# Fourteen of 22 inner tiles of the first feed-forward layer by seven block products instead of eight

## The chip, the cores and the metric

The kernel runs on one core of a Trainium2 chip. Its engines are TensorE (PE, with its weight loads shown apart as PEld), VectorE (DVE), ScalarE (ACT), GpSimd (POOL) and SyncE (SP), each with an instruction queue of its own; SP, ACT and POOL can also issue DMAs. The time is the device time of one launch in microseconds; less is better.

## The reference

Four layers work on a residual stream `x` of 512 tokens and 1024 features, each on an RMS norm of it: a Conformer convolution module, a feed-forward layer (the one that is changed), four-head retention with rotary positions, and a second feed-forward layer. All is float32.

```python
def conv_ffn(x, w_in, dw_w, dw_b, w_out):
    h = x @ w_in                          # 1024 -> 2 x 2816
    a, u = jnp.split(h, 2, axis=-1)
    a = causal_dwconv(a, dw_w, dw_b)      # three taps along the tokens
    return (jax.nn.silu(a) * u) @ w_out   # 2816 -> 1024

h = rmsnorm(x, norm_ffn_g[i])
x = x + conv_ffn(h, ffn_w_in[i], ffn_dw_w[i], ffn_dw_b[i], ffn_w_out[i])
```

The retention layer turns its queries and keys by `cos` and `sin` of position times inverse frequency, two tables of 128 x 512.

## The kernel before

The stream lies transposed in SBUF, as eight tiles `xT` of 128 features x 512 tokens. Every float32 product is made as three products in the format fp32r: a factor is split into a high part (cast to fp32r) and a low part (the rest), and `mm3` adds high x high, low x high and high x low into one PSUM bank (lines L272 to L274 when a helper of the scheduler records them, and L279 to L283 in the conv layer). Of the weights, ACT makes the high part `wh` (L229) and DVE the low part `wl` (L233), 128 x 1024 at a time, from a raw chunk `wr` of 128 x 2048 (1 MB) that SP's queue loads. `wr`, `wh` and `wl` have four buffers each. `weights()` gives the factors of one chunk (a "unit") to the products and emits the split of the unit after it.

The inner width 2816 of a feed-forward layer is 22 tiles of 128. `HALVES` cuts them in two groups, 0 to 12 and 12 to 22. `ffn_half` takes the tiles of a group: per tile f one bank `fa` and one bank `fu`, each of 8 blocks of features x 3 matmuls with all 512 tokens moving, so 48 matmuls a tile and 96 for a pair of tiles, which shares two chunks of weights. The norm's factor per token is not in the moving factor `n1x` (only the gain is): it is multiplied in when a bank is emptied (`evac`, L811 to L820):

- `ap` = `fa` x `n1r` on DVE (L812), after POOL has zeroed two columns ahead of it (L811);
- the last tap with bias on ACT (L814), the two others on DVE (L815, L816), silu on ACT (L817), times `n1r` on POOL (L818);
- `fy` = `fu` x `ft` on DVE (L820), and its split into `y…h` on ACT (L348) and `y…l` on DVE (L349).

After each group `proj_out` multiplies the `y` tiles by `ffn_w_out` (banks `fo`) and DVE adds the result to `xT` (L430).

The norm's sums are made while the conv layer's output products (`co`, partly with 256 tokens a matmul) run: ACT squares each new `xT` tile (L379), POOL adds six of the eight squares (L380, `n1acc`), and a short chain gives the factor per token: `n1v` on DVE (L330), a power on POOL (L314, `n1y`), a diagonal on DVE (L336, `n1d`), two products that spread it over all partitions (L339, bank `n1b`) and an ACT copy to `n1r` (L341). `n1b` stands among the first products of the layer.

`rotary_tables` (L843 to L877) is a generator. The first feed-forward layer steps it once per tile, behind that tile's L818 and L820. Nearly all of its instructions are POOL's.

The order of the instructions on each engine is set by the Tile framework's scheduler, from its own estimates; `tc.issue_after(i)` keeps an instruction behind another. Heads 1 to 3 of the retention layer already make their values and gates by seven products, with weight sums added by DVE (L255).

Of the kernel before, what the change touches and what calls it, by code (L numbers as in the profile page):

```python
# [74 lines left out]
def _chunks():  # L75


    out, blocks = [], []
# [70 lines left out]
def trunk(ctx, tc, xt_d, positions, ret_gn_g, final_g, weights_d, cols_d, mats_d, ident_d, decay_d, invf_d, out):  # L149
# [30 lines left out]
    chunks, squares = _chunks()  # L180
    descs = [(nk, sum(n for _, n in ranges)) for _, _, _, nk, ranges in chunks]

    units, i = [], 0
    while i < len(descs):
        units += [(i, n) for n in range(7)] if i in squares else [(i, None)]
        i += 4 if i in squares else 1
# [248 lines left out]
    ss0 = sp.tile([P, 1], F32, tag="ss0", bufs=1, name="ss0")
    with conv_scope:
# [298 lines left out]
        def step_v(_, half):  # L735
# [6 lines left out]
            for i in range(KD):  # L742
# [18 lines left out]
                latest[0] = act.copy(hi, c)  # L761
# [20 lines left out]
        proj_out(zs, "co", n1, between=lambda k: run(SEQ_OUT.get(k, "")))  # L782


    def ffn_half(fp, l, norm, f0, f1, hooks=(), side=None):
# [18 lines left out]
        def evac(f):  # L804
            pa, pu = mid.pop(f)

            def wc(j):
# [5 lines left out]
            t = fp.tile([P, S], F32, tag="ft", bufs=3, name=f"ft{l}_{f}")  # L813
            act.activation(t, ap[:, 2:], AF.Identity, scale=wc(2), bias=wc(3))  # L814
            dve.scalar_tensor_tensor(out=t, in0=ap[:, 1:1 + S], scalar=wc(1), in1=t, op0=ALU.mult, op1=ALU.add)  # L815
            dve.scalar_tensor_tensor(out=t, in0=ap[:, 0:S], scalar=wc(0), in1=t, op0=ALU.mult, op1=ALU.add)  # L816
            act.activation(t, t, AF.Silu)  # L817
# [15 lines left out]
    cos = cp.tile([P, S], F32, name="cos")
    sin = cp.tile([P, S], F32, name="sin")

    def rotary_tables(rp):

        posi = rp.tile([P, S], I32, tag="r0", name="posi")
        act.dma_start(posi, positions.partition_broadcast(P))
        invf = cp.tile([P, 1], F32, name="invf")  # L840
        act.dma_start(invf, invf_d)
        ang = rp.tile([P, S], F32, tag="r1", name="ang")
        pool.tensor_copy(ang, posi)  # L843
        pool.tensor_scalar(out=ang, in0=ang, scalar1=invf, scalar2=None, op0=ALU.mult)
        c = [rp.tile([P, S], F32, tag=f"rc{j}", name=f"rc{j}") for j in range(3)]
        dve.tensor_scalar(out=c[0].bitcast(I32), in0=ang.bitcast(I32), scalar1=-65536, scalar2=None, op0=ALU.bitwise_and)
        pool.tensor_tensor(out=ang, in0=ang, in1=c[0], op=ALU.subtract)
        dve.tensor_scalar(out=c[1].bitcast(I32), in0=ang.bitcast(I32), scalar1=-65536, scalar2=None, op0=ALU.bitwise_and)
        pool.tensor_tensor(out=c[2], in0=ang, in1=c[1], op=ALU.subtract)
        q = inv_two_pi_parts()  # L850
        turn = rp.tile([P, S], F32, tag="r2", name="turn")
        p = rp.tile([P, S], F32, tag="r0", name="prod")
        n = rp.tile([P, S], F32, tag="r1", name="near")

        def turns(dst, src):
            pool.tensor_scalar(out=n, in0=src, scalar1=MAGIC, scalar2=-MAGIC, op0=ALU.add, op1=ALU.add)  # L856
            pool.tensor_tensor(out=dst, in0=src, in1=n, op=ALU.subtract)

        yield
        first = True  # L860
        for j, parts in ((0, 4), (1, 3), (2, 3)):
            for i in reversed(range(parts)):
                pool.tensor_scalar(out=p, in0=c[j], scalar1=q[i], scalar2=None, op0=ALU.mult)
                if (i, j) == (0, 0):
                    turns(p, p)
                if first:
                    turns(turn, p)
                    first = False
                else:
                    turns(p, p)  # L870
                    pool.tensor_tensor(out=turn, in0=turn, in1=p, op=ALU.add)
                yield
        turns(turn, turn)
        act.activation(sin, turn, AF.Sin, scale=TWO_PI)
        pool.tensor_scalar(out=turn, in0=turn, scalar1=0.25, scalar2=None, op0=ALU.add)
        turns(turn, turn)
        act.activation(cos, turn, AF.Sin, scale=TWO_PI)  # L877
# [416 lines left out]
```

## Time and profile before

| what | value |
|---|---|
| time, median of 3 runs | 1293.81 us (1292.75 to 1294.05) |
| the profiled execution's own time | 1293.24 us |
| its span in the profile | 1291.5 us |
| granted TensorE clock, mean | 0.999 of full speed |
| first of the conv layer's output products `co` | 136.2 us from the span's start |
| first and last start of the first feed-forward layer's `fa` products (their first block of features) | 182.3 and 477.9 us |

A row of the timeline gives the start, the duration, the engine, the line, the operation, out<-in and, in brackets, the idle time of the engine just before and what ended it. A row of the groups gives line, engine, operation, out<-in, the count, the summed time in us with the mean in ns, and the idle time ahead of it. PE's matmuls overlap, so the rate is read from their starts and not from their durations.

### The profile page before, as it was taken

The numbers are of one execution on the slowest core, as the hardware profiler recorded it, in microseconds if no ns is written. First come the engines' busy times: TensorE is split into PE (matmuls) and PEld (weight loads), VectorE is DVE, ScalarE is ACT, GpSimd is POOL, SyncE is SP. The second block draws the span as 40 slices with busy tenths as digits, with TensorE's granted clock in tenths as the row PEclk, the third lists the DMA queues.
The fourth block names the chain that finished last, engine by engine and source line by source line (L and its number), as shares of the span: only waits on it lengthen the run. The fifth ranks groups of instructions, "written<-read, shape, count | busy, mean of one in ns | idle before, by whom it ended". The sixth has DMA issues, their size and how long they took to land.

```text
span 1291.5 us, 15110 instructions
## 1 busy us (share of the span) xinstructions
PE 1282.0 (99%) x5955; PEld 1067.0 (83%) x5955; DVE 810.0 (63%) x1036; ACT 520.9 (40%) x703; POOL 355.2 (28%) x305
## 2 busy tenths in 40 slices
PE   9999999999999999999999999999999999999997
PEld 7889988888888888888888888878888888888886
DVE  6998657665335554579696596596675643355542
ACT  6646644333124333334435335354443431233332
POOL 0957323797006110221311312304211110011111
PEclk9999999999999999999999999999999999999999
DMA  9533422313221313323314405323224342213111
GB/s 330 225 123 106 148 98 70 127 66 130 98 98 66 130 49 114 131 81 106 106 42 160 138 14 180 103 83 116 97 76 145 94 143 98 98 66 131 33 65 65
DMA packets 35926, 140.48 MB, mean 109 GB/s; under 512 B 10896, under 2 KB 15760, under 8 KB 21776
## 3 DMA queue, kind: packets, MB, share of 16 engines
q1 hardware_dynamic: 32256, 134.02, 30.2%
q10 hardware_dynamic: 3600, 5.52, 1.5%
q8 instruction: 46, 0.75, 0.2%
q14 instruction: 24, 0.20, 0.0%
HBM read 130.08 MB, written 2.10 MB: 102 GB/s over the span
## 4 chain that ended last, share of the span: by engine, by line
PE 96%; DVE 2%; issue 1%; ACT 0%; POOL 0%; POOLq 0%
PE fa L272 6%; PE fa L274 6%; PE fu L273 6%; PE fu L272 6%; PE fu L274 6%; PE fa L273 6%; PE lo L272 3%; PE fo L273 3%; PE fo L274 3%; PE lo L273 3%; PE lo L274 3%; PE fo L272 3%; PE cph L539 2%; PE ro L272 2%; PE ro L273 2%; PE ro L274 2%
## 5 line engine op out<-in xcount | busy, mean ns | idle before, releaser
L233 DVE TENSOR_TENSOR wl<-wr,wh 128x1024 fp32r<-128x1024 f32 (+2 forms) x242 | 302.7, 1254 | 207.2 <-ACT wh L229 203.7
L229 ACT CAST wh<-wr 128x1024 fp32r<-128x1024 f32 (+2 forms) x244 | 250.5, 1029 | 372.0 <-PE fo L274 82.7
L811 POOL MEMSET ap<- 128x2 f32 x44 | 4.2, 99 | 371.7 <-DVE ft L816 305.4
L988 POOL TENSOR_TENSOR gg<-gg,gn 128x512 f32<-128x512 f32 x16 | 27.5, 1719 | 179.3 <-ACT gg L987 179.3
L820 DVE TENSOR_TENSOR fy<-fu,ft 128x512 f32<-128x512 f32 x44 | 30.4, 690 | 68.6 <-PE fu L274 35.0
L814 ACT ACTIVATE ft<-ap,prm 128x512 f32<-128x512 f32 x44 | 35.8, 814 | 71.3 <-DVE ap L812 71.3
L588 DVE SCALAR_TENSOR_TENSOR tp<-hp,prm,tp 128x512 f32<-128x512 f32 x80 | 55.8, 747 | 0.4
L579 POOL TENSOR_TENSOR pla<-pla,plt 128x512 f32<-128x512 f32 x36 | 49.1, 1365 | 9.8 <-ACT pla L575 5.7
L815 DVE SCALAR_TENSOR_TENSOR ft<-ap,prm,ft 128x512 f32<-128x512 f32 x44 | 37.2, 844 | 17.7 <-ACT ft L814 17.5
L817 ACT ACTIVATE ft<-ft 128x512 f32<-128x512 f32 x44 | 27.9, 633 | 45.0 <-DVE ft L816 44.6
L972 POOL TENSOR_TENSOR rs<-rs 128x512 f32<-128x512 f32 x16 | 24.7, 1559 | 67.5 <-DVE rs L971 43.7
L818 POOL TENSOR_TENSOR ft<-ft,n3r 128x512 f32<-128x512 f32 x22 | 32.1, 1461 | 29.0 <-ACT ft L817 29.0
L818 POOL TENSOR_TENSOR ft<-ft,n1r 128x512 f32<-128x512 f32 x22 | 31.6, 1434 | 28.8 <-ACT ft L817 28.8
L816 DVE SCALAR_TENSOR_TENSOR ft<-ap,prm,ft 128x512 f32<-128x512 f32 x44 | 35.8, 814 | 1.5
L578 ACT ACTIVATE plt<-hp,prm 128x512 f32<-128x512 f32 x36 | 25.8, 722 | 20.6 <-POOL pla L579 20.2
L539 PEld LDWEIGHTS cph<-ph,cmat 128*128 128x128 f32 x288 | 32.6, 192 | 0.2
L539 PE MATMUL cph<-ph,cmat 128*128 128x128 f32 x288 | 32.6, 275 | 0.0
L430 DVE TENSOR_TENSOR xT<-ro,xT 128x512 f32<-128x512 f32 x32 | 21.6, 682 | 15.6 <-PE ro L274 15.6
L255 DVE TENSOR_TENSOR wr<-wr,wr 128x1024 f32<-128x1024 f32 x24 | 28.8, 1211 | 0.0
L812 DVE TENSOR_TENSOR ap<-fa,n3r 128x512 f32<-128x512 f32 x22 | 15.1, 690 | 20.5 <-PE fa L274 20.5
L812 DVE TENSOR_TENSOR ap<-fa,n1r 128x512 f32<-128x512 f32 x22 | 15.1, 689 | 17.2 <-PE fa L274 17.2
L856 POOL TENSOR_SCALAR near<-prod 128x512 f32<-128x512 f32 x11 | 22.9, 2085 | 0.9
(1851 smaller groups left out, 3842.1 us busy)
## 6 DMA issues: line engine op xcount, KB each, us to landing
wr<-in_weights_dram SPq DMA_DIRECT2D x106, 1024.0 KB, 4.9
cmat<-in_mats_dram SPq DMA_DIRECT2D x4, 2304.0 KB, 10.6
wr<-in_weights_dram SPq DMA_DIRECT2D x4, 512.0 KB, 3.4
wr<-in_weights_dram SPq DMA_DIRECT2D x6, 256.0 KB, 6.8
yt<-yq ACTq DMA_DIRECT2D x24, 64.0 KB, 2.1
yt<-yq SPq DMA_DIRECT2D x24, 64.0 KB, 2.1
xt<-xq SPq DMA_DIRECT2D x32, 48.0 KB, 2.0
xT<-in_xt_dram SPq DMA_DIRECT2D x4, 256.0 KB, 4.4
```

Of the source, the lines that this page charges most:

```text
L229: latest[0] = act.copy(hi[:, o:o + n], raw[:, s + o:s + o + n])
L233: latest[1] = low_on.get(i, dve).tensor_tensor(out=lo[:, o:o + n], in0=raw[:, s + o:s + o + n], in1=hi[:, o:o + n].bitcast(F32), op=ALU.su ...
L272: pe.matmul(ps, wh, xh, start=first, stop=False, **check)
L273: pe.matmul(ps, wl, xh, start=False, stop=False, **check)
L274: pe.matmul(ps, wh, xl, start=False, stop=last, **check)
L539: pe.matmul(ps[:, g * P:(g + 1) * P], mats[i][g][:, s, :], ph[:, g, NSH - 1 - s:NSH - 1 - s + P], start=s == 0, stop=s == NSH - 1)
L579: gate[0] = pool.tensor_tensor(out=pl, in0=pl, in1=tm, op=ALU.add).ins
L588: dve.scalar_tensor_tensor(out=a, in0=hp[:, t:t + S], scalar=tap(t, i), in1=a, op0=ALU.mult, op1=ALU.add)
L814: act.activation(t, ap[:, 2:], AF.Identity, scale=wc(2), bias=wc(3))
L815: dve.scalar_tensor_tensor(out=t, in0=ap[:, 1:1 + S], scalar=wc(1), in1=t, op0=ALU.mult, op1=ALU.add)
L816: dve.scalar_tensor_tensor(out=t, in0=ap[:, 0:S], scalar=wc(0), in1=t, op0=ALU.mult, op1=ALU.add)
L818: scaled = pool.tensor_tensor(out=t, in0=t, in1=norm.rb, op=ALU.mult)
```

## The change

The second feed-forward layer keeps its two groups. The first has three: tiles 0 to 8 as before, 8 to 14 and 14 to 22 by blocks, two tiles at a time:

- **Seven products instead of eight.** The features are cut in two (blocks 0 to 3 and 4 to 7) and so are the tokens (256 and 256). The weights of a pair of tiles come in two chunks: the first holds, for the first four blocks of features, the columns of `a` (w11) and then those of `u` (w12), the second the same for the other four (w21, w22). Strassen's scheme in Winograd's form gives the four blocks of the result from seven products x11, x12, s1, s2, s3, x22, s4, each of 2 tiles x 4 blocks of features x 3 matmuls with 256 tokens, 24 matmuls, so 168 a pair. Three banks are used (z, x, p); z takes x11, s2, s3 and x22 one on top of the other, and ACT copies it out in between (`q1`, `u1`, `u2`, L919).
- **Sums of the weights.** Each of the seven factors is one unit of 128 x 1024 with one cast and one subtraction (now L239, L243). Three of them are sums, made in place in the raw chunks by `pair_factor`: one DVE addition (L282), two DMAs that POOL issues and that add what they read from the weights in DRAM to SBUF (L283, L285), and one that adds one part of SBUF to another (L286).
- **Sums of the tokens.** The norm's factor is multiplied into `x` here (L873 on in the new class `Factors`), so there is no multiplication by `n1r` behind these products. The sums s1 to s4 and the split of the normed `x` are made during the first group.
- **Emptying.** `ap` from bank x plus `q1` (DVE, L932) and from z (ACT, L944), `fy` from p less `u2` and less `u1` (DVE, L940 and L948), the taps as before (L959 to L962), then `fy` x `ft` (L949) and the split (L377, L378). Three output products `fo0`, `fo1` and `fo2` take the place of two: their matmuls are as many as before, DVE's additions to `xT` eight more.
- **Rotary tables.** They are emitted right behind the conv layer's output products, in the conv layer's scope, and most of what was a POOL multiplication or rounding is now DVE's; the subtractions and additions stay with POOL (L477 to L502).

```diff
-HALVES = [(0, 12), (12, 22)]
+GROUPS = [[(0, 8, False), (8, 14, True), (14, 22, True)], [(0, 12, False), (12, 22, False)]]
...
+                if by_blocks:
+                    pairs.append(len(out))
+                    for kc in range(2):
+                        cols("ffn_w_in", l, 512 * kc, 4, (f * P, 256), (F + f * P, 256), apart=True)
...
+    def pair_factor(i, n):
+        if n == 0:
+            for j in (i, i + 1):
+                next(load_weights(j))
+        w11, w12 = raws[i][:, :1024], raws[i][:, 1024:]
+        w21, w22 = raws[i + 1][:, :1024], raws[i + 1][:, 1024:]
+        if n == 2:
+            dve.tensor_tensor(out=w11, in0=w11, in1=w12, op=ALU.add)
+            pool.dma_start(w12, weights_d[i + 1, :, 1024:], accum_op=ALU.add)
+        if n == 3:
+            pool.dma_start(w11, weights_d[i + 1, :, 1024:], accum_op=ALU.add)
+            pool.dma_start(w21, w11, accum_op=ALU.add)
+        return (w11, w21, w11, w11, w12, w21, w22)[n]
...
+    def rotary_tables(temps, act_behind, pool_behind):
...
+        def turns(dst, src, n):
+            dve.tensor_scalar(out=n, in0=src, scalar1=MAGIC, scalar2=-MAGIC, op0=ALU.add, op1=ALU.add)
+            pool.tensor_tensor(out=dst, in0=src, in1=n, op=ALU.subtract)
+        terms = [(j, i) for j, parts in ((0, 4), (1, 3), (2, 3)) for i in reversed(range(parts))]
+        for m, (j, i) in enumerate(terms):
+            p, n = ps[m % 2], ns[m % 2]
+            dve.tensor_scalar(out=p, in0=c[j], scalar1=q[i], scalar2=None, op0=ALU.mult)
...
+            turns(p if m else turn, p, n)
+            if m:
+                pool.tensor_tensor(out=turn, in0=turn, in1=p, op=ALU.add)
...
         proj_out(zs, "co", n1, between=lambda k: run(SEQ_OUT.get(k, "")))
+        rotary_tables(cv.tile([P, PH, NM], F32, tag="cmat", bufs=2, name="rotary").rearrange("p a n -> p (a n)"),
+                      ends_v["act"], ends_v["pool"])
...
+    class Factors:
+        def sums_of(self, k):
+            x1, x2 = self.normed(k), self.normed(k + 4)
...
+            dve.tensor_tensor(out=a[:, 0], in0=x1[:, hi], in1=x2[:, hi], op=ALU.subtract)
+            dve.tensor_tensor(out=a[:, 1], in0=a[:, 0], in1=x1[:, lo], op=ALU.subtract)
+            dve.tensor_tensor(out=b[:, 0], in0=x1[:, lo], in1=x1[:, hi], op=ALU.subtract)
+            dve.tensor_tensor(out=b[:, 1], in0=x2[:, lo], in1=a[:, 1], op=ALU.add)
+            for o, t in ((0, a), (2, b)):
+                h, l = (u[:, k, o:o + 2, :] for u in self.sums)
+                act.copy(h, t)
+                dve.tensor_tensor(out=l, in0=t, in1=h.bitcast(F32), op=ALU.subtract)
...
+    def ffn_blocks(fp, l, norm, f0, f1, left):
+        for f in range(f0, f1, 2):
...
+            z = bank("z")
+            product(z, "x11", True)
+            q1 = kept(z, "q1")
+            x = bank("x")
+            product(x, "x12", True)
+            for j in range(2):
+                dve.memset(aps[j][:, :2], 0.0)
+                dve.tensor_tensor(out=aps[j][:, 2:2 + N2], in0=x[j], in1=q1[j], op=ALU.add)
+            p = bank("p")
+            product(p, "s1", True)
+            product(z, "s2")
+            u1 = kept(z, "u1")
+            product(z, "s3")
+            u2 = kept(z, "u2")
+            for j in range(2):
+                dve.tensor_tensor(out=us[j][:, hi], in0=p[j], in1=u2[j], op=ALU.subtract)
+            product(z, "x22")
+            ts = []
+            for j in range(2):
+                act.copy(aps[j][:, 2 + N2:2 + S], z[j])
+                ts.append(taps(fp, l, f + j, aps[j]))
+            product(p, "s4")
+            for j in range(2):
+                dve.tensor_tensor(out=us[j][:, lo], in0=p[j], in1=u1[j], op=ALU.subtract)
+                dve.tensor_tensor(out=us[j], in0=us[j], in1=ts[j], op=ALU.mult)
+                ys.append(split(us[j], f"y{l}_{f + j}", ("yh", "yl"), fp))
+        return ys
```

The order on DVE where a pair's last tiles meet the next pair's weights. Before (`wl22` and `wl23` are the low parts of the next pair's chunks):

```order
L812 TENSOR_TENSOR ap0_8_2588<-fa0_8_2469,n1r_1923 128x512
L815 SCALAR_TENSOR_TENSOR ft0_8_2591<-ap0_8_2588,prm_95,ft0_8_2591 128x512
L816 SCALAR_TENSOR_TENSOR ft0_8_2591<-ap0_8_2588,prm_95,ft0_8_2591 128x512
L820 TENSOR_TENSOR fy0_8_2597<-fu0_8_2494,ft0_8_2591 128x512
L349 TENSOR_TENSOR y0_8l_2600<-fy0_8_2597,y0_8h_2599 128x512
L233 TENSOR_TENSOR wl22_0_2462<-wr22_2459,wh22_0_2461 128x1024
```

Now, on the same engine, where tiles 8 and 9 end (`wr26` and `wr27` are the raw chunks of tiles 10 and 11, `wl31` to `wl37` their seven low parts):

```order
L282 TENSOR_TENSOR wr26_3048<-wr26_3048 128x1024
L940 TENSOR_TENSOR fy0_9_2839<-fp0_9_2911,u20_9_3003 128x256
L243 TENSOR_TENSOR wl32_0_3099<-wr27_3050,wh32_0_3098 128x1024
L960 SCALAR_TENSOR_TENSOR ft0_8_3037<-ap0_8_2836,prm_95,ft0_8_3037 128x512
L961 SCALAR_TENSOR_TENSOR ft0_8_3037<-ap0_8_2836,prm_95,ft0_8_3037 128x512
L931 MEMSET ap0_10_3092 128x2
L948 TENSOR_TENSOR fy0_8_2838<-fp0_8_2910,u10_8_2970 128x256
L243 TENSOR_TENSOR wl33_0_3135<-wr26_3048,wh33_0_3134 128x1024
```

The low part of the third factor, `wl33`, stands behind L948, which reads the last product (s4) of the pair before; L285 overwrites what `wl33` reads.

On ACT, in the same place, before (casts of the next chunk between the taps of two tiles):

```order
L814 ACTIVATE ft0_8_2591<-ap0_8_2588,prm_95 128x512
L817 ACTIVATE ft0_8_2591<-ft0_8_2591 128x512
L348 CAST y0_8h_2599<-fy0_8_2597 128x512
L229 CAST wh22_0_2461<-wr22_2459 128x1024
L229 CAST wh22_1024_2465<-wr22_2459 128x1024
```

Now (`fz0_10` is bank z of the next pair, `wh34` to `wh37` the casts of its last four factors):

```order
L919 COPY q10_10_3126<-fz0_10_3096 128x256
L919 COPY q10_11_3127<-fz0_11_3097 128x256
L377 CAST y0_8h_3082<-fy0_8_2838 128x512
L962 ACTIVATE ft0_9_3043<-ft0_9_3043 128x512
L239 CAST wh34_0_3170<-wr26_3048 128x1024
L239 CAST wh35_0_3198<-wr26_3048 128x1024
L377 CAST y0_9h_3088<-fy0_9_2839 128x512
L239 CAST wh36_0_3230<-wr27_3050 128x1024
L239 CAST wh37_0_3264<-wr27_3050 128x1024
L919 COPY u10_10_3226<-fz0_10_3096 128x256
```

All seven casts stand ahead of the copy `u1`, which frees bank z for the product s3.

On POOL, around the norm's power (L314, now L343). Before:

```order
L380 TENSOR_TENSOR n1acc_1310<-n1acc_1310,n1sq4_1777 128x512
L380 TENSOR_TENSOR n1acc_1310<-n1acc_1310,n1sq5_1785 128x512
L380 TENSOR_TENSOR n1acc_1310<-n1acc_1310,n1sq6_1793 128x512
L314 TENSOR_TENSOR n1y_1892<-n1v_1889,minus_half_92 128x4
```

Now:

```order
L409 TENSOR_TENSOR n1acc_1312<-n1acc_1312,n1sq6_1795 128x512
L497 TENSOR_TENSOR rotary_1806<-rotary_1806 128x512 x2
L487 TENSOR_TENSOR rotary_1806<-rotary_1806 128x512 x2
L497 TENSOR_TENSOR rotary_1806<-rotary_1806 128x512 x2
L487 TENSOR_TENSOR rotary_1806<-rotary_1806 128x512
L343 TENSOR_TENSOR n1y_1948<-n1v_1945,minus_half_92 128x4
```

Of the rotary tables' 128 x 512 operations, 17 stand between the first `n1acc` and `n1y`.

More of the change, by code (lines that the diff above doesn't have):

```diff
@@ L128, in _chunks @@
     ffn(1)
-    return out, blocks
+    return out, blocks, pairs
 LINE = 256
@@ L177, in pe_in_order @@
         return tc.issue_after(next(i for i in reversed(nc.cur_bb.bb.instructions) if i.engine == mybir.EngineType.PE))
[L180 to L181 removed]
+    chunks, squares, pairs = _chunks()
+    descs = [(nk, sum(n for _, n in ranges)) for _, _, _, nk, ranges, _ in chunks]
     units, i = [], 0
     while i < len(descs):
[L185 to L186 removed]
+        many = 4 if i in squares else 2 if i in pairs else 1
+        units += [(i, n) for n in range(7)] if many > 1 else [(i, None)]
+        i += many
     state = {"emitted": 0, "used": 0}
@@ L242, in emit_weights @@
         i, n = units[unit]
+        if i in pairs:
+            for _ in split_raw(pair_factor(i, n), i, unit):
+                pass
+            return
         if n is None:
@@ new lines, in ffn_blocks, with bank, product, kept @@
+    def ffn_blocks(fp, l, norm, f0, f1, left):
+        ys = []
+        for f in range(f0, f1, 2):
+            def bank(which):
+                return [psum(f"f{which}{l}_{f + j}")[:, :N2] for j in range(2)]
+            def product(pss, which, first=False):
+                w = weights()
+                for j, ps in enumerate(pss):
+                    for k, (xh, xl) in enumerate(left.factor(which)):
+                        mm3(ps, *w(k, j * P, (j + 1) * P), xh, xl, first and k == 0, k == 3, skip_group_check=not first)
+            def kept(pss, name):
+                tiles = [fp.tile([P, N2], F32, tag=name, bufs=2, name=f"{name}{l}_{f + j}") for j in range(2)]
+                for t, ps in zip(tiles, pss):
+                    act.copy(t, ps)
+                return tiles
+            lo, hi = slice(0, N2), slice(N2, S)
+            aps = [fp.tile([P, S + 32], F32, tag="ap", bufs=2, name=f"ap{l}_{f + j}") for j in range(2)]
+            us = [fp.tile([P, S], F32, tag="fy", bufs=2, name=f"fy{l}_{f + j}") for j in range(2)]
+            z = bank("z")
[25 more added lines that the diff above has]
+        return ys
@@ new lines, in taps, with wc @@
+    def taps(fp, l, f, ap):
+        def wc(j):
+            return fw[l][:, j * NF + f:j * NF + f + 1]
+        t = fp.tile([P, S], F32, tag="ft", bufs=3, name=f"ft{l}_{f}")
+        act.activation(t, ap[:, 2:2 + S], AF.Identity, scale=wc(2), bias=wc(3))
+        dve.scalar_tensor_tensor(out=t, in0=ap[:, 1:1 + S], scalar=wc(1), in1=t, op0=ALU.mult, op1=ALU.add)
+        dve.scalar_tensor_tensor(out=t, in0=ap[:, 0:S], scalar=wc(0), in1=t, op0=ALU.mult, op1=ALU.add)
+        act.activation(t, t, AF.Silu)
+        return t
@@ L786, in ffn_half @@
+    def ffn_half(fp, l, norm, f0, f1, hooks=(), side=None, each=None):
         ys, wt, mid = [], {}, {}
@@ L812, in evac @@
             dve.tensor_tensor(out=ap[:, 2:], in0=pa, in1=norm.rb, op=ALU.mult)
[L813 to L817, printed above, removed]
+            t = taps(fp, l, f, ap)
             scaled = pool.tensor_tensor(out=t, in0=t, in1=norm.rb, op=ALU.mult)
@@ L829, in ffn_half @@
             evac(f - 1)
+            if each is not None:
+                next(each, None)
         evac(f1 - 1)
         return ys
[L833 to L871, printed above, removed]
-                yield
[L873 to L877, printed above, removed]
@@ L1023, in product @@
                 for tb in range(2):
-                    for k, (xh, xl) in enumerate(left(which)):
+                    for k, (xh, xl) in enumerate(left.factor(which)):
                         t = slice(tb * P, (tb + 1) * P)
```

143 lines of the change are left out of this document (84 added, 59 removed).

## Prediction

> **What bounds the kernel now.** I read the page's engine totals first, then the chain of waits, then the feed-forward layer's groups.
>
> ```profile
> PE 1282.0 (99%) x5955; PEld 1067.0 (83%) x5955; DVE 810.0 (63%) x1036; ACT 520.9 (40%) x703; POOL 355.2 (28%) x305
> PE 96%; DVE 2%; issue 1%; ACT 0%; POOL 0%; POOLq 0%
> ```
>
> TensorE is busy nearly throughout, the chain runs over it, and the clock stands at 0.999: time goes only when matmul time goes, and comes where PE is made to wait. So the change has one gain (fewer matmul-microseconds) and I look for places where it starves PE. PE's price per matmul I take from starts, first for 512 moving tokens (first and last of 25 starts in a row), then for 256 (first of the first and first of the last of 17 rows that hold four matmuls each).
>
> ```profile
> 205.47 0.39 PE L272 MATMUL fa<-n1x0h,wh 128*128 128x512 f32 x1
> ...
> 210.91 0.39 PE L272 MATMUL fu<-n1x0h,wh 128*128 128x512 f32 x1
> ```
> ```profile
> 136.73 0.64 PE L281 MATMUL co<-z0h,wl 128*128 128x256 f32 x4
> ...
> 144.40 0.64 PE L283 MATMUL co<-z5l,wh 128*128 128x256 f32 x4
> ```
>
> The first is 5.44 us for 24, 0.2267 us each; the second 7.67 for 64, 0.120 each, although every matmul has a new stationary factor whose load shows 190 ns.
>
> **Matmuls.** A pair of tiles gives up 96 x 0.2267 = 21.76 us and takes 168 x 0.120 = 20.16: seven eighths of the work at a rate 6% worse. The gain is 1.60 a pair, 11.2 us for seven pairs. The output products keep their matmuls; a third group adds only eight DVE additions beside work.
>
> **Busy time of the other engines per pair.** Durations from before:
>
> ```profile
> L233 DVE TENSOR_TENSOR wl<-wr,wh 128x1024 fp32r<-128x1024 f32 (+2 forms) x242 | 302.7, 1254 | 207.2 <-ACT wh L229 203.7
> L229 ACT CAST wh<-wr 128x1024 fp32r<-128x1024 f32 (+2 forms) x244 | 250.5, 1029 | 372.0 <-PE fo L274 82.7
> L255 DVE TENSOR_TENSOR wr<-wr,wr 128x1024 f32<-128x1024 f32 x24 | 28.8, 1211 | 0.0
> L820 DVE TENSOR_TENSOR fy<-fu,ft 128x512 f32<-128x512 f32 x44 | 30.4, 690 | 68.6 <-PE fu L274 35.0
> L815 DVE SCALAR_TENSOR_TENSOR ft<-ap,prm,ft 128x512 f32<-128x512 f32 x44 | 37.2, 844 | 17.7 <-ACT ft L814 17.5
> L588 DVE SCALAR_TENSOR_TENSOR tp<-hp,prm,tp 128x512 f32<-128x512 f32 x80 | 55.8, 747 | 0.4
> L814 ACT ACTIVATE ft<-ap,prm 128x512 f32<-128x512 f32 x44 | 35.8, 814 | 71.3 <-DVE ap L812 71.3
> L817 ACT ACTIVATE ft<-ft 128x512 f32<-128x512 f32 x44 | 27.9, 633 | 45.0 <-DVE ft L816 44.6
> L758 DVE TENSOR_TENSOR cs<-lnbb,cs 128x256 f32<-128x256 f32 x6 | 2.4, 418 | 0.1
> L761 ACT CAST z3h<-cs 128x256 fp32r<-128x256 f32 x2 | 0.8, 406 | 0.1
> ```
>
> DVE: 7 subtractions of 1.23, one addition of 1.21, 4 taps of 0.75 (the conv layer's row of the same operation, since POOL, which stands beside the 0.84 of L815, is now nearly empty; at 0.84 it is 0.4 more), 4 of 512 columns at 0.69, 6 of 256 at 0.4: 18.2 us of 20.16. ACT: 7 casts of 1.03, 8 copies of 0.41, 2 x (0.81 + 0.63 + 0.62): 14.7. Neither bounds by its sum; DVE keeps 2 us to spare, so what counts is the order.
>
> **The chain that binds in a pair.** Place t = 0 at its first product; each product takes 2.88 us. On DVE the low part `wl33` stands behind L948, which waits for the last pair's s4: the first of its two tiles is done half a product earlier, about t = -1.28 with the hand-over. L948 takes 0.36 and `wl33` 1.22 (to 0.30). Only then may L285 overwrite w11, then L286 read it, one DMA after the other, Δ each. Behind them on ACT come casts `wh36` and `wh37` and then the copy `u1`, which the fifth product, s3, needs at 4 x 2.88 = 11.52. A cast holds ACT for 0.94 and a hand-over takes 0.04, by these rows:
>
> ```profile
> 170.69 1.04 ACT L229 CAST wh<-wr 128x1024 fp32r<-128x1024 f32 x1
> 171.63 0.72 ACT L351 ACTIVATE n1x2h<-xT,prm 128x512 fp32r<-128x512 f32 x1
> ```
> ```profile
> 196.62 1.05 ACT L229 CAST wh<-wr 128x1024 fp32r<-128x1024 f32 x1 [10.84 <-PE fa L274]
> 197.71 1.23 DVE L233 TENSOR_TENSOR wl<-wr,wh 128x1024 fp32r<-128x1024 f32 x1 [1.13 <-ACT wh L229]
> ```
>
> With 0.2 for the hand-overs, `u1` is out at 0.30 + 2Δ + 1.90 + 0.41 + 0.20 = 2Δ + 2.81: PE waits 2Δ - 8.7 us in each of the five pairs that follow a pair. In the first pair of a group DVE isn't held by an s4, and I give it 1.1 less (2Δ - 9.8). Queued behind a late cast on ACT are also `wh38` and the copies `u2`; behind a late `wl36` on DVE stand `wl37` and L940. These inherit the delay but add none, since z is late by as much.
>
> No DMA that adds, and none that POOL issues, runs before. The nearest rows:
>
> ```profile
> wr<-in_weights_dram SPq DMA_DIRECT2D x106, 1024.0 KB, 4.9
> wr<-in_weights_dram SPq DMA_DIRECT2D x4, 512.0 KB, 3.4
> yt<-yq ACTq DMA_DIRECT2D x24, 64.0 KB, 2.1
> ```
>
> Lower end 3.2 to 3.4 (a plain 512 KB transfer); upper end 2 x 3.4 = 6.8 (read and write one after the other). I take 4.85, the row in which 1 MB is moved, since an adding DMA reads the 512 KB that come and the 512 KB that are there. Then PE waits 2 x 4.85 - 8.7 = 1.0 us in five pairs, and -0.1, so nothing, in two: +5.0. At 3.4 it is nothing; at 6.8 it would be 5 x 4.9 + 2 x 3.8 = 32.
>
> The Trainium skill, "Collectives: The Full Stack", Part 3, has a DMA's addition cost a second read of its source rather than arithmetic, and "DMA: Bandwidth & Descriptors", section on the anatomy of one DMA, fits POOL-issued transfers as 2.0 us plus the bytes over 436 GB/s; for 1 MB read that makes an estimate of 4.4 us, a wait of 0.1 a pair and a time of about 1284.5. No run here shows it; my sum goes by the row of 4.85.
>
> **The first group.** It now also holds the sums of the tokens: DVE 18.2 us for s1 to s4 and 11.5 for the eight normed splits (by the same rows), less the rotary work.
>
> ```profile
> 205.20:292.40 87.20, 87.20 (x386) 72.19 (x386) 58.76 (x63) 33.84 (x43) 61.62 (x47) 1.00 0.27 93
> ```
>
> In this stretch, just as long as the new first group (8 tiles x 48 x 0.2267 = 87 us), DVE works 58.8 of 87.2 us (the fourth number; ACT 33.8, POOL 61.6). That leaves 28 us, and the group's output products, 8 x 8 x 3 x 0.2267 = 43.5 us more, come before the first x11 needs anything of it: hidden, cost 0. If the splits were late they would delay x11 of tile 8; DVE's work would have to grow by tens of microseconds first.
>
> **The rotary tables.** They leave the layer, where they were hidden, and stand on POOL between the squares' sums and the norm's power `n1y`.
>
> ```profile
> L871 POOL TENSOR_TENSOR turn<-turn,prod 128x512 f32<-128x512 f32 x9 | 15.2, 1694 | 0.5
> L857 POOL TENSOR_TENSOR prod<-prod,near 128x512 f32<-128x512 f32 x10 | 14.4, 1440 | 0.8
> L380 POOL TENSOR_TENSOR n1acc<-n1acc,n1sq 128x512 f32<-128x512 f32 x6 | 8.7, 1447 | 23.8 <-ACT n1sq L379 23.7
> 164.51 4.96 POOL L380 TENSOR_TENSOR n1acc<-n1acc,n1sq 128x512 f32<-128x512 f32 x3 [14.09 <-ACT n1sq L379]
> 194.82 1.03 POOL L314 TENSOR_TENSOR n1y<-n1v,minus_half 128x4 f32<-128x4 f32 x1 [11.87 <-DVE n1v L330]
> 195.88 0.69 DVE L336 TENSOR_TENSOR n1d<-ident,n1y 128x512 f32<-128x512 f32 x1 [1.14 <-POOL n1y L314]
> 199.15 1.02 PE L339 MATMUL n1b<-n1d,ones 128*128 128x512 f32 x2
> ```
>
> From 164.51 on POOL has, before `n1y`, 6 sums x 1.447 + 11 subtractions x 1.44 + 6 additions x 1.694 = 34.7 us, so `n1y` starts about 199.2 instead of 194.82, and `n1d` is ready 1.03 + 0.69 + 0.04 later, 200.95. PE asks for `n1b` at 199.15: a wait of 1.8 us. Bounds: 0, if all 23 take 1.36 us or POOL begins earlier than 164.5; 23 x 1.694 = 39.0 from the dearest row gives 6.1. I take 1.8, the rows' own durations. The 26 DVE operations lie beside PE; one that waits for POOL is at most an operation late, with the splits of `n1x` behind it, which PE meets later than that.
>
> Removed at the same time: the rotary operations of the first tiles and 14 multiplications by `n1r`, all off the path: 0. The seven pairs' weights come as 1 MB chunks as before, plus 14 x 0.5 MB read a second time; DMA stands at 0.27 busy (the number before the last in the stretch above): 0. A pair holds two of the four `wr` buffers until its last cast; the two others take the next pair's loads, 4.9 us against a lead of some 20: 0. On POOL the three DMAs of a pair wait in its queue, and nothing but the next pair's stands behind them.
>
> **Sum.** -11.2 + 5.0 + 1.8 = -4.4 us. The profiled execution took 1293.24, 0.57 under the median of 1293.81, so I forecast 1288.8 to 1289.4: 1289.
>
> **Rivals.**
> - *The adding DMAs are wholly hidden* (Δ up to 4.35): -11.2 + 1.8 = -9.4, some 1284. For it speaks the 3.4 row; against it, the second operand that has to be fetched. The two pages named above come out on this side.
> - *The adding DMAs starve PE* and the kernel is slower. At Δ = 6.0, under the upper end: 5 x 3.3 + 2 x 2.2 = 20.9, less 11.2, plus 1.8: some 1305. Slower than 1293.8 from 5 x (2Δ - 8.7) + 2 x (2Δ - 9.8) = 9.4, Δ = 5.2; so only 0.35 over the value I take. For it speaks that two of them stand in series each pair with ACT's casts behind. Here the Trainium skill, "SBUF — State Buffer", the section on who interferes with whom, speaks against the change: a POOL-issued DMA has its descriptors written by POOL, which a DVE operation in a two-port mode locks out; it exempts additions and subtractions of two tensors, which are nearly all of DVE's work here, and no trace of before shows one.
> - *POOL's queue ahead of `n1y`* at its dear end, 6.1 instead of 1.8, or DVE's 18.2 stretched by a tenth to the pair's 20.16: some 1293 to 1294, no change.
> - *256-token matmuls dearer than 0.120*: the `co` rows leave no room; put into the range.
>
> **How the numbers follow.** Forecast (Δ about 4.6 to 5.05, own range 1285.5 to 1292): 0.40. Hidden: 0.22. Starved: 0.27. POOL or DVE: 0.11. A measurement of this kernel tells 0.2%, 2.6 us, from no change. Faster by more takes the hidden case and most of the forecast's: 0.54. Slower takes the starved case and a little of POOL's: 0.31. Within: 0.15. The range reaches from 1282 (hidden, no wait at `n1y`) to 1303 (Δ about 5.9), leaving out the worse half of the starved case.
>
> **What would show it.** L285 and L286 from issue to landing: near 4.85 I'm right, under 4.4 the hidden rival, over 5.2 the slow one. A pair's x11 to the next x11 should be 21.2 us, 20.2 without a wait; PE's idle time should stand ahead of s3, with a cast or `u1` as releaser. `n1b` should show 1 to 2 us of idle time on PE, released by `n1d`. DVE should be 90% busy in the pairs. Wrong would I be above all in Δ, each 0.1 us of which is some 1.0 us (five pairs) to 1.4 us (seven) of time.

## The result, and the profile after

The changed kernel takes 1325.19 us (median of 4 runs, 1323.60 to 1327.19) against 1293.80 (4 runs, 1292.75 to 1294.05): ratio 1.0245, 95% interval 1.0227 to 1.0263. It is 31.4 us slower. The prediction was 1289, with a range to 1303: wrong in the sign and outside the range. First the page after, the same parts as before (totals, chain), then the DMAs that POOL issues:

```profile
PE 1285.3 (97%) x6459; PEld 1089.5 (82%) x6459; DVE 896.8 (68%) x1186; ACT 566.6 (43%) x796; POOL 312.4 (24%) x274
PE 79%; DVE 9%; issue 7%; DMA 2%; POOL 2%; ACT 1%; POOLq 0%; ACTq 0%; DVEq 0%
wr<-in_weights_dram POOLq DMA_DIRECT2D x14, 512.0 KB, 5.9
wr<-wr POOLq DMA_DIRECT2D x7, 512.0 KB, 4.6
```

PE's share of the chain falls from 96% to 79%: PE waits now. Its waits in the profile after (who waits, for what: us in all, times, the longest):

```profile
PE fz L301 <- ACT u L919: 12.4, 6, 2.3
PE fz L302 <- DVE wl L243: 4.5, 6, 0.8
PE fa L303 <- DVE n1x4l L381: 3.6, 1, 3.6
PE n1b L368 <- DVE n1d L365: 2.6, 1, 2.6
PE fa L301 <- ACT n1x4h L380: 2.2, 1, 2.2
```

Two places, then: the pairs (bank z: products s2 and s3) and the first products of the layer. The layer in stretches (bounds; length; busy time of PE, PEld, DVE, ACT, POOL; granted clock; DMA share), from its first `fa` to `fo0`, `fo0`, the first group of pairs with `fo1`, the second with `fo2`:

```profile
182.36:288.32 105.96, 96.00 (x391) 75.62 (x390) 91.81 (x120) 43.61 (x60) 45.07 (x36) 0.94 0.23 80
288.32:331.84 43.52, 43.52 (x193) 36.05 (x192) 27.05 (x36) 13.75 (x17) 2.40 (x2) 1.00 0.36 109
331.84:437.02 105.18, 96.70 (x650) 89.40 (x648) 65.22 (x87) 46.47 (x69) 8.69 (x10) 0.98 0.53 137
437.02:574.65 137.63, 127.91 (x866) 118.63 (x865) 87.13 (x115) 69.73 (x106) 16.04 (x16) 0.99 0.52 141
```

Without waits the pairs' two stretches would be 7 x 20.16 + (6 + 8) x 8 x 3 x 0.2267 = 217.3 us; they take 242.8, so 25.5 are lost there. The first stretch takes 106.0; a run below without its waits takes 88.4, so 17.6 are lost there. With the matmuls' -11.2 that is +31.9, and the time rose by 31.4. Not all of it is idle time. PE waits for some 10 us in the first stretch and 18 in the pairs (the rows above and smaller ones); a part of the rest is a granted clock of one half for 3.5 to 8.2 us after some waits (0.50 from 191.8 to 199.5 us). The same length of wait (1.96 us ahead of s3) is followed by it in one pair and not in the next.

**Where the pairs' chain goes.** One of the pairs, from the low part of the third factor to s3 (timeline of DVE, POOL, ACT and PE):

```profile
483.24 1.22 DVE L243 TENSOR_TENSOR wl<-wr,wh 128x1024 fp32r<-128x1024 f32 x1
484.86 0.86 POOL L285 DMA_DIRECT2D wr<-in_weights_dram  x1 [5.88 <-DVE wl L243]
490.65 2.00 ACT L239 CAST wh<-wr 128x1024 fp32r<-128x1024 f32 x2 [3.09 <-DMA wr<-in_weights_dram]
491.03 0.87 POOL L286 DMA_DIRECT2D wr<-wr  x1 [5.30 <-DMA wr<-in_weights_dram]
493.01 0.39 PE L302 MATMUL fz<-n1sh,wl 128*128 128x256 f32 x1 [0.76 <-DVE wl L243]
495.67 1.99 ACT L239 CAST wh<-wr 128x1024 fp32r<-128x1024 f32 x2 [2.50 <-DMA wr<-wr]
497.57 0.64 ACT L919 COPY u<-fz 128x256 f32<-128x256 f32 x2
497.99 0.39 PE L301 MATMUL fz<-n1sh,wh 128*128 128x256 f32 x1 [2.08 <-ACT u L919]
```

It is the predicted chain, step for step: `wl33`, L285, L286, two casts, the copy, s3. It holds s2 up too, which needs what L285 leaves.

**Where the first stretch goes.** DVE and POOL, 189 to 192 us, and first the same kind of split at 182 us, where POOL is idle:

```profile
182.16 0.74 DVE L381 SCALAR_TENSOR_TENSOR n1x3l<-xT,prm,n1x3h 128x512 fp32r<-128x512 f32 x1
...
188.93 1.11 DVE L486 TENSOR_SCALAR rotary<-rotary 128x512 f32<-128x512 f32 x1
189.72 1.45 POOL L409 TENSOR_TENSOR n1acc<-n1acc,n1sq 128x512 f32<-128x512 f32 x1
189.96 1.75 DVE L381 SCALAR_TENSOR_TENSOR n1x4l<-xT,prm,n1x4h 128x512 fp32r<-128x512 f32 x1
191.13 1.72 POOL L487 TENSOR_TENSOR rotary<-rotary 128x512 f32<-128x512 f32 x1
191.63 1.76 DVE L381 SCALAR_TENSOR_TENSOR n1x5l<-xT,prm,n1x5h 128x512 fp32r<-128x512 f32 x1
```

`n1x3l`, with POOL idle, takes 0.74; `n1x4l`, which starts while POOL works, 1.75: POOL's operation ends at 191.17, and DVE's 0.54 later. From there the two engines take turns, and a split's 0.74 becomes 1.75 for `n1x4l`, `n1x5l` and `n1x6l`. The addition to `xT`, which takes one of its inputs from a PSUM bank, keeps its 0.68 although POOL works all the while:

```profile
192.81 1.73 POOL L409 TENSOR_TENSOR n1acc<-n1acc,n1sq 128x512 f32<-128x512 f32 x1
193.32 0.68 DVE L459 TENSOR_TENSOR xT<-co,xT 128x512 f32<-128x512 f32 x1
```

The Trainium skill, "SBUF — State Buffer", the section "Who interferes with whom", says that a DVE instruction with two inputs in SBUF contends with a POOL instruction that reads SBUF; these rows agree. The prediction quoted that section for DMA descriptors and passed over this sentence of it.

### The profile page after: what moved, and what is told of

It is laid out like the page before. It is cut to its first block, busy times and chain, and to the rows that moved or that the text cites. A ratio compares the mean times of both kernels' runs of the same rounds, so it can differ in the third digit from the quotient of the medians.

```text
span 1322.9 us, 16374 instructions
## 1 busy us (share of the span) xinstructions
PE 1285.3 (97%) x6459; PEld 1089.5 (82%) x6459; DVE 896.8 (68%) x1186; ACT 566.6 (43%) x796; POOL 312.4 (24%) x274
## 4 chain that ended last, share of the span: by engine, by line
PE 79%; DVE 9%; issue 7%; DMA 2%; POOL 2%; ACT 1%; POOLq 0%; ACTq 0%; DVEq 0%
PE fu L303 3%; PE fu L302 3%; PE fu L301 3%; PE fa L302 3%; PE fa L303 3%; PE fa L301 3%; PE fo L301 3%; PE fo L303 3%; PE fo L302 3%; PE lo L302 3%; PE lo L303 3%; PE lo L301 3%; PE cph L609 2%; DVE wl L243 2%; PE qk L302 2%
## 5 line engine op out<-in xcount | busy, mean ns | idle before, releaser
L243 DVE TENSOR_TENSOR wl<-wr,wh 128x1024 fp32r<-128x1024 f32 (+2 forms) x263 | 328.9, 1259 | 189.8 <-ACT wh L239 186.9
L239 ACT CAST wh<-wr 128x1024 fp32r<-128x1024 f32 (+2 forms) x265 | 271.4, 1032 | 348.9 <-PE lo L302 70.9
L959 ACT ACTIVATE ft<-ap,prm 128x512 f32<-128x512 f32 x44 | 35.9, 818 | 42.7 <-DVE ap L988 42.1
L992 DVE TENSOR_TENSOR fy<-fu,ft 128x512 f32<-128x512 f32 x30 | 20.7, 689 | 40.8 <-POOL ft L990 22.2
L301 PE MATMUL fz<-n1sh,wh 128*128 128x256 f32 x112 | 33.3, 306 | 13.7 <-ACT u L919 12.4
L960 DVE SCALAR_TENSOR_TENSOR ft<-ap,prm,ft 128x512 f32<-128x512 f32 x44 | 34.3, 782 | 13.3 <-ACT ft L959 13.2
L962 ACT ACTIVATE ft<-ft 128x512 f32<-128x512 f32 x44 | 27.8, 632 | 28.3 <-DVE ft L961 27.8
L302 PE MATMUL fz<-n1sh,wl 128*128 128x256 f32 x112 | 33.4, 301 | 4.5 <-DVE wl L243 4.5
L301 PEld LDWEIGHTS fz<-n1sh,wh 128*128 128x128 f32 x112 | 22.3, 203 | 15.8 <-ACT u L919 13.6
L283 POOL DMA_DIRECT2D wr<-in_weights_dram x7 | 6.3, 904 | 121.4 <-DVE wr L282 89.2
L648 ACT ACTIVATE plt<-hp,prm 128x512 f32<-128x512 f32 x36 | 25.9, 725 | 20.6 <-POOL pla L649 20.1
L961 DVE SCALAR_TENSOR_TENSOR ft<-ap,prm,ft 128x512 f32<-128x512 f32 x44 | 32.9, 750 | 1.0
L303 PE MATMUL fz<-n1sl,wh 128*128 128x256 f32 x112 | 32.7, 294 | 0.0
## 6 DMA issues: line engine op xcount, KB each, us to landing
cmat<-in_mats_dram SPq DMA_DIRECT2D x4, 2304.0 KB, 11.2
```

What stands on the lines that cost most here:

```text
L239: latest[0] = act.copy(hi[:, o:o + n], raw[:, s + o:s + o + n])
L243: latest[1] = low_on.get(i, dve).tensor_tensor(out=lo[:, o:o + n], in0=raw[:, s + o:s + o + n], in1=hi[:, o:o + n].bitcast(F32), op=ALU.su ...
L301: pe.matmul(ps, wh, xh, start=first, stop=False, **check)
L302: pe.matmul(ps, wl, xh, start=False, stop=False, **check)
L303: pe.matmul(ps, wh, xl, start=False, stop=last, **check)
L959: act.activation(t, ap[:, 2:2 + S], AF.Identity, scale=wc(2), bias=wc(3))
```

## The experiments

All times are medians beside runs of the kernel before on the same chip (1293.5 to 1293.7).

### Each half undone

`rot_only` is the kernel before with the rotary part of the change's diff and nothing else. The three others edit the changed kernel. `sum_dve`:

```diff
         if n == 3:
-            pool.dma_start(w11, weights_d[i + 1, :, 1024:], accum_op=ALU.add)
+            dve.tensor_tensor(out=w11, in0=w11, in1=w22, op=ALU.add)
             pool.dma_start(w21, w11, accum_op=ALU.add)
```

`rot_back` makes the tables in the first group again, with POOL, in three temporaries and the two tables' own tiles; `both` has both edits:

```diff
-        rotary_tables(cv.tile([P, PH, NM], F32, tag="cmat", ...), ends_v["act"], ends_v["pool"])
...
+        rotary = rotary_tables(fp)      # a generator again, turns() on POOL
...
-                ys = ffn_half(fp, 0, n1, f0, f1, (None, n1.stats, n1.bcast), each=sums_of_x())
+                ys = ffn_half(fp, 0, n1, f0, f1, (None, n1.stats, n1.bcast), rotary, each=sums_of_x())
...
             proj_out(ys, f"fo{n}", n2)
+            if not by_blocks:
+                for _ in rotary:
+                    pass
```

> The kernel before with nothing of the change but the rotary tables behind the conv layer's output products. Theory (the tables hold DVE and POOL against each other while the norm's splits are due, PE waits about 10 us in the first eight tiles and its clock then drops for some 7 us more): 1293.8 + 17 = 1311 us (1306 to 1314), waits ahead of the second half of n1x in the first fa product and ahead of n1b. Rival (the tables cost only the queue on POOL ahead of n1y, as predicted): 1293.8 + 1.8 to 2.6 = 1296. Rival (the loss in the first group comes from the sums of the tokens and not from the tables): 1294.

> The changed kernel with the rotary tables made during the first eight tiles on POOL, as before the change (in three temporaries and the two tables themselves). Theory: the first group's loss of 17 us goes, 1325.2 - 17 = 1308 us (1305 to 1312); the waits in the pairs stay. Rival (only POOL's queue ahead of n1y): 1325.2 - 2.6 = 1322.6. Rival (sums of the tokens are the cause): 1325.

> The changed kernel with the third sum (w11 + w22) added by DVE in 1.2 us instead of by a DMA of 5.8 us and its issue; the other DMAs stay. Theory (in the pairs PE waits for a chain of two adding DMAs in series): the chain gets 5 us shorter, more than the 3.3 us that PE waits in a pair, so all 25 us of the pairs go: 1325.2 - 25 = 1300 us (1299 to 1306). Rival (DVE or ACT is the pairs' bound, 17 to 18 us of work in 20): DVE gets 1.2 us more a pair, 1325 to 1333.

> The two edits together: rotary tables back in the first group and the third sum on DVE. Theory: what is left of the change is the matmuls' gain, 1293.8 - 11.2 = 1282.6 us (1281 to 1288), faster than the kernel before. Rival (DVE bounds the pairs): 1308 or more. Rival (the matmuls of 256 tokens cost more than 0.120 us in the pairs): 1294, no change.

Measured: `rot_only` 1309.05 us (ratio to before 1.0121, interval 1.0104 to 1.0138), so the rotary move alone costs 15.4 us (17 expected); its waits are those of the changed kernel:

```profile
PE n1b L339 <- DVE n1d L336: 4.0, 1, 4.0
PE fa L274 <- DVE n1x4l L352: 3.6, 1, 3.6
PE fa L272 <- ACT n1x4h L351: 2.2, 1, 2.2
```

The sums of the tokens, which this kernel doesn't have, are therefore not the cause. `sum_dve` 1304.25 (1.0082, 1.0067 to 1.0097): 21 of the pairs' 25 us go though DVE has more to do, so DVE isn't their bound. What stays is the copy ahead of s3:

```profile
PE fz L301 <- ACT u L919: 3.6, 5, 0.8
```

`rot_back` 1315.42 (1.0166, 1.0150 to 1.0181) gains 9.8 instead of 17, and `both` 1294.72 (1.0010, 1.0001 to 1.0019) only reaches the time before. In `rot_back` and `both` the first stretch is down to 88.7 us, but `fo0` takes 48.6 instead of 43.5 and waits for the last tile:

```profile
PE fo L303 <- DVE y_7l L378: 2.3, 1, 2.3
```

The rows of `both` show why it is late:

```profile
278.76 1.40 POOL L992 TENSOR_TENSOR ft<-ft,n1r 128x512 f32<-128x512 f32 x1 [2.11 <-ACT ft L964]
280.64 2.31 DVE L243 TENSOR_TENSOR wl<-wr,wh 128x1024 fp32r<-128x1024 f32 x1
285.17 0.68 DVE L994 TENSOR_TENSOR fy<-fu,ft 128x512 f32<-128x512 f32 x1
```

POOL's multiplication of tile 7 by `n1r` (L992) isn't held up by rotary work: POOL stood idle for 2.11 us before it. But DVE comes to tile 7's product L994 only 5.0 us after that multiplication has ended, 12.3 us after the first matmul of `fo0`; in `both2` below, whose tables need no POOL, it is 6.5 us after it. DVE's operations are drawn out beside POOL's rotary operations (L243 takes 2.31 us in the row above, 1.21 at 277.13 with POOL idle). The rotary work also runs over into the first pairs. The place was bad; that the tables could have a free place was still open.

### What is dear in it

`plain` leaves `accum_op` out of L285 and L286, which make the fourth and the sixth factor. `filler` puts needless matmuls where PE waits. `rot_nopool` drops POOL's rotary subtractions L487 and additions L497; in the place of two of them, where a tile would otherwise not be written, it has a multiplication on DVE (L488). `both2` has three edits: the sum by DVE, the order of two casts on ACT, and the tables made by DVE alone behind output products.

```diff
# filler, in mm() of the first product, ahead of k = 4
+                        for _ in range(24):
+                            last = pe.matmul(spare, wt[which](0, o, o + P)[0], norm.xs[0][0], start=True, stop=True)
# both2, the order on ACT: a cast is issued behind the copy that is named here
+                with tc.issue_after(late_cast[0]) if late_cast[0] else ...:
                     latest[0] = act.copy(hi[:, o:o + n], raw[:, s + o:s + o + n])
...
             u1 = kept(z, "u1")
+            late_cast[0] = copied[0]        # the first of u1's two copies
             product(z, "s3")
+            late_cast[0] = None
             u2 = kept(z, "u2")
+            late_cast[0] = copied[0]        # of u2's
...
             product(z, "x22")
+            late_cast[0] = None
# both2, in proj_out: a step of the tables (all on DVE) behind every second bank
+                        if side is not None and c % 2:
+                            with tc.issue_after(latest[1].ins):
+                                next(side, None)
```

> The changed kernel with its DMAs L285 and L286 copying instead of adding (so the third and sixth factors are not the sums they should be; queues, sizes, order and waits stay). Theory A (the addition makes the transfer dear, by a second read): L285 falls from 5.9 us to landing to about 4.5, L286 from 4.6 to about 3.5, the chain gets 2.5 us shorter and six pairs with it: 1325.2 - 15 = 1310 us (1306 to 1316). Rival (what is dear is that POOL issues them): both landings and the time stay, 1325.

> The changed kernel with 24 needless matmuls of 512 tokens (5.4 us) into a spare bank in the middle of the first fa product, where PE waits 5.8 us for n1x4. Theory (the clock drops to half because PE stood idle there): the needless work lies in the wait, the clock stays at 1.0 from 188 to 200 us, and the kernel gets 4 to 5 us faster: 1320.5 us (1318 to 1323). Rival (the clock drops for another reason, or the wait only moves): 1325 to 1331.

> The changed kernel with POOL's share of the rotary sum (the subtractions L487 and additions L497) left out, so that the tables are wrong, and DVE's share kept in its place. Theory (POOL's operations and DVE's operations with two operands in SBUF shut each other out, so that each waits for the other): DVE's operations fall back to 0.42 and 0.74 us, the waits ahead of n1x4 and n1b go: 1325.2 - 15 = 1310 us (1308 to 1313). Rival (DVE simply has 11 us more to do there): 1320 or more.

> The changed kernel with the third sum on DVE, with the casts of the last two factors behind the copies u1 and u2 on ACT, and with the rotary tables made by DVE alone, a step behind each second bank of the output products fo0 and fo1. Theory: the waits of 0.7 to 0.8 us ahead of s3, and the 5 us that the first group and fo0 lost in the run with both edits, go, and the matmuls' 11.2 us are left as the gain: 1283 us (1281 to 1288). Rival (DVE is the pairs' bound, or the tables cost as much wherever they stand): 1290 to 1295.

`plain`: 1299.55 us (1.0048, 1.0030 to 1.0066), more than expected: L285 falls to 3.9 us to landing and L286 to 2.9, and with 3.7 us less in the chain no pair waits at all (length of the pairs and their output products, PE busy in all of it):

```profile
331.65:549.28 217.63, 217.63 (x1513) 204.24 (x1512) 151.75 (x202) 116.91 (x175) 20.15 (x26) 1.00 0.48 155
```

So of the landing times 2.0 and 1.7 us are the addition; L283, which still adds here, stays at 5.9. The page "Collectives: The Full Stack" of the Trainium skill, Part 3, says of the reduce step of a collective that its addition costs a second source read and not cycles of the adder; these runs show the 2.0 and 1.7 and can't tell a read from an addition. The fit on the page "DMA: Bandwidth & Descriptors" of the Trainium skill gave an estimate of 4.4 us for 1 MB; 5.9 was measured with an addition.

`filler`: 1326.38 (1.0256, 1.0240 to 1.0272); the rival was right. The 24 matmuls did lie in the wait and the clock did stay up, but PE then waited for `n1x5l` to `n1x7l`, and the clock fell at 198 instead of 190:

```profile
185.60 5.60 PE L982 MATMUL spare<-n1x0h,wh 128*128 128x512 f32 x24
191.04 0.39 PE L301 MATMUL fa<-n1x4h,wh 128*128 128x512 f32 x1
...
197.99 0.77 PE L303 MATMUL fa<-n1x6l,wh 128*128 128x512 f32 x1 [2.93 <-DVE n1x6l L381]
```

DVE's splits set the pace there; a PE at half speed met them just in time. So it is not right to count the half clock of that place as a cost of its own, as the expectations did.

`rot_nopool`: 1314.34 (1.0156, 1.0138 to 1.0174), 10.9 of the 15 expected. DVE's operations are short again except beside POOL's sums `n1acc`, which remain (L488 below takes 1.51), but `n1x4l` still comes late:

```profile
188.85 0.41 DVE L486 TENSOR_SCALAR rotary<-rotary 128x512 f32<-128x512 f32 x1
189.18 0.74 DVE L381 SCALAR_TENSOR_TENSOR n1x4l<-xT,prm,n1x4h 128x512 fp32r<-128x512 f32 x1
189.85 1.51 DVE L488 TENSOR_SCALAR rotary<-rotary 128x512 f32<-128x512 f32 x1
```

The first stretch takes 96.3 us here: of its 17.6 us, 9.7 go with POOL's operations, and 7.9 stay, with rotary operations ahead of the splits in DVE's own queue. Of these 7.9, some is due to POOL's remaining sums (two L486 beside them take 2.68 us together) and to the added L488; no run separates that. Both theories held in part.

`both2`: 1282.08 us (0.9910, 0.9895 to 0.9926), 11.6 us faster than the kernel before. Nothing waits in the layer (the three stretches: first group, `fo0`, pairs with `fo1` and `fo2`):

```profile
182.87:271.27 88.40, 88.40 (x392) 72.85 (x390) 68.85 (x100) 40.14 (x54) 11.93 (x15) 1.00 0.26 89
271.27:314.79 43.52, 43.52 (x194) 36.04 (x192) 40.77 (x65) 12.85 (x16) 2.38 (x2) 1.00 0.31 98
314.79:532.11 217.32, 217.32 (x1514) 204.12 (x1512) 163.86 (x226) 118.35 (x177) 18.60 (x19) 1.00 0.49 139
```

Their sum is 349.2 us; the same stretch before is

```profile
182.33:542.75 360.42, 360.42 (x1592) 298.07 (x1590) 190.97 (x208) 124.71 (x151) 122.59 (x98) 1.00 0.28 97
```

and the difference is the matmuls' 11.2.

### The edits one by one

`rot_fo` has only the tables' new place, `copy_first` only the order on ACT, `sum_order` that order and the sum by DVE. `dma_par`:

```diff
             pool.dma_start(w12, weights_d[i + 1, :, 1024:], accum_op=ALU.add)
+            pool.dma_start(w21, w11, accum_op=ALU.add)
         if n == 3:
             pool.dma_start(w11, weights_d[i + 1, :, 1024:], accum_op=ALU.add)
-            pool.dma_start(w21, w11, accum_op=ALU.add)
+            pool.dma_start(w21, weights_d[i + 1, :, 1024:], accum_op=ALU.add)
```

> The changed kernel with only the rotary tables moved: made by DVE alone behind the banks of fo0 and fo1, nothing of them ahead of the norm. The weights' DMAs stay. Theory: the first group takes 88.4 us from its first product to fo0 instead of 106.0, the pairs keep their waits: 1325.2 - 17.5 = 1307.7 us (1305 to 1311). Rival (the tables cost the same wherever DVE makes them): 1318 or more.

> The changed kernel with only the order on ACT changed: the cast of the sixth factor stands behind the copy u1 and that of the seventh behind u2. No DMA gets shorter. Theory (what waits ahead of s3 is the copy behind the casts that wait for L286): the 2.2 us ahead of s3 go with the clock's drops that follow them, the 1.1 us ahead of s2 stay: six pairs, 1325.2 - 13 to 18 = 1307 to 1312 us. Rival (the wait moves on to x22, which needs the same factor): 1318 to 1325.

> The changed kernel with four adding DMAs a pair instead of three and no two of the late ones in series: w21 takes w11 + w12 early and then w22 from DRAM beside L285. Theory (the two late DMAs in series bind): the casts for s3's copy come 4 us earlier, the wait ahead of s3 goes and that ahead of s2 stays, since L285 is as late as before: 1307 to 1312 us. Rival (a fourth adding DMA slows the others down in proportion): no gain, 1320 to 1330.

> The changed kernel with the third sum on DVE and with ACT's order of the run copy_first; the rotary tables stay in the conv layer. Theory: the pairs wait for nothing, 20.16 us each, and only the first group's 17.5 us remain: 1293.8 - 11.2 + 17.5 = 1300 us (1298 to 1302), 4 to 5 less than with the sum alone (1304.3). Rival (DVE's 18 us in 20 a pair keep a wait): 1304.

`rot_fo` 1306.42 us (1.0098, 1.0083 to 1.0113): the first stretch takes 88.4, as expected. `sum_order` 1299.60 (1.0047, 1.0031 to 1.0064): the pairs wait for nothing. With the matmuls these account for the result: 1325.2 less 18.8 (`rot_fo`) and 25.6 (`sum_order`) make 1280.8, and `both2`, which is the two together, took 1282.1.

`copy_first` 1319.67 (1.0199, 1.0184 to 1.0215) gains 5.5 instead of 13 to 18. The wait ahead of s3 is gone, but that ahead of s2 grew:

```profile
PE fz L303 <- ACT wh L239: 7.8, 5, 2.2
PE fz L304 <- DVE wl L243: 4.3, 6, 0.8
```

The scheduler had moved the third factor's low part (`wl33` in the first pair) behind two taps on DVE, so the DMA of L285 was issued later. I had taken the order as given; an edit on one engine changed it on another.

`dma_par` 1350.16 (1.0437, 1.0421 to 1.0452), 25 us slower still. The premise was wrong: the DMA that adds w22 to w11 must wait until the early one has read w11, so that two adding DMAs stand in series as before, and the last two run at once and take 7.9 and 5.9 us to land (medians):

```profile
PE fz L302 <- ACT wh L239: 31.2, 6, 6.3
```

## Why the prediction was wrong, point by point

- **Matmuls, -11.2:** right, in size too (`both2`: 349.2 against 360.4).
- **The chain that binds in a pair, +5.0:** the right chain, mis-sized; the pairs lost 25.5. A pair took some 3.5 us more in place of 1.0. Of these 2.5, some 0.75 are the DMAs (5.8 and 4.6 to landing in place of 2 x 4.85), some 0.6 the issue on POOL, 0.40 and 0.38 us between each releaser and its DMA, where I had 0.2 in all for hand-overs. The largest part, 1.1, could have been read before: in the changed kernel's order on PE nine matmuls of the next pair's x11 (eleven in some pairs) stand ahead of s4, 9 x 0.12 us, so that L948 and `wl33` come that much later against the work that PE has left:

```
L303 MATMUL fz0_16_4056<-n1n7l_2587,wh61_0_4190 128x256
L302 MATMUL fz0_18_4312<-n1n0h_2544,wl63_0_4269 128x256
L303 MATMUL fz0_18_4312<-n1n0l_2545,wh63_0_4268 128x256
...
L301 MATMUL fp0_16_4126<-n1sh_1868,wh62_0_4224 128x256
```

  (`fz0_16` is x22, `fz0_18` the next pair's x11, `fp0_16` s4.) And of the pairs that start a group, which I gave nothing, the first lost 4.7 us and the second none. The half clock after waits, 3.5 us long in two pairs and so 1.7 us of time in each, was in no term. The starved rival (5.2 and up) had the right sign and place but took Δ alone as its cause; with the measured mean, 5.25, my sum still came out at some 1295, no change.
- **The rotary tables, +1.8:** this step failed. It counted POOL's queue ahead of `n1y` and set DVE's 26 operations and the splits behind them at nothing, "at most an operation late". `rot_only` measured 15.4. Two things were missing: DVE's and POOL's operations shut each other out (0.74 to 1.75 us), and DVE, which takes its queue in order, has the splits `n1x4l` to `n1x7l` behind rotary operations. The rows of before showed the first: `n1x5l` beside one of POOL's additions, which ended at 182.95:

```profile
182.16 1.34 DVE L352 SCALAR_TENSOR_TENSOR n1x5l<-xT,prm,n1x5h 128x512 fp32r<-128x512 f32 x1 [0.39 <-ACT n1x5h L351]
```

  The wait that the step did forecast came, 2.6 us ahead of `n1b` for 1.8, but that the size is near is luck. `n1y` started at 209.47 and not at 199.2, and PE asked for `n1b` at 209.96 (212.51 less the wait of 2.55) and not at 199.15, since it had lost time before. Nor was POOL's queue the last to hold it: on DVE `n1v` stood behind rotary operations, of which one had waited 3.68 us for POOL, and `n1y` waited for `n1v`:

```profile
205.80 0.43 DVE L492 TENSOR_SCALAR rotary<-rotary 128x512 f32<-128x512 f32 x1 [3.68 <-POOL rotary L497]
207.58 0.68 DVE L358 TENSOR_REDUCE n1v<-n1s 128x4 f32<-128x512 f32 x1
209.47 1.20 POOL L343 TENSOR_TENSOR n1y<-n1v,minus_half 128x4 f32<-128x4 f32 x1 [0.44 <-DVE n1v L359]
```

- **The first group's sums, 0:** right; `both2` has them in a stretch of 88.4 us with PE busy throughout.
- **The rival that DVE, stretched, fills the pairs:** wrong, but not by much. In `both2`, with an addition more, DVE works 17.5 of 20.1 us in the pair from 338.06 to 358.20, and PE waits for nothing. The estimate of DVE's work was near (its terms, as rounded there, add up to 18.0 and not 18.2). The 163.9 of 217.3 us in the row of `both2` above are lower because `fo1` and `fo2` lie in them.

## What to carry to other kernels

A gain of a few per cent in matmul time is there only if every step of the chain that feeds it fits, and the room is read from the order of the changed kernel on all engines, PE's included, not from the order that the code suggests. Before work is moved beside other work on DVE and POOL, look for a row where the two overlap: an operation that doubles its time is dearer than its own duration. A DMA that adds in place saves an engine's time, but stands in the chain for as long as a plain one and here 1.7 to 2.0 us more; one DVE addition of 1.2 us with 2 us to spare was the better choice.

## What the runs showed of the hardware

A POOL-issued DMA of 512 KB landed in 3.9 us from DRAM and 2.9 from SBUF without an addition, in 5.9 and 4.6 with one, and of two adding DMAs at once one took 7.9. A DVE operation with two inputs in SBUF took 1.75 us instead of 0.74 beside POOL's operations; one with an input in PSUM kept its 0.68. A wait of PE of 2 to 6 us was in some cases followed by 3 to 8 us at a granted clock of 0.50; at 256 tokens a matmul then took 0.21 us instead of 0.12. In `filler` the clock stayed up until 198 us and PE waited for DVE instead, at 1326.4 us in place of 1325.2; what a clock that stays up throughout would be worth there was not tried.
